# First stage of an encoder block: modulation weights loaded ahead of x, weight splits moved to VectorE, products of ones on TensorE

## The chip, the core and the metric

One core of a Trainium2 chip runs one launch of the kernel. The metric is the device time of one execution in microseconds, and the kernel before is given by the median of three: 2219.39 us (2219.05 to 2223.93).

TensorE multiplies matrices, VectorE, ScalarE and GpSimd (POOL in the profile) work elementwise, SyncE (SP) issues nearly all DMAs. Each engine takes its own instructions strictly in the order of the program and waits for the others by semaphores.

## The reference

A block of three residual steps on x (1024 tokens by 1024 channels, float32): a SwiGLU feed-forward, a mixer (chunked attention beside a recurrent branch), and a second SwiGLU feed-forward. Before each step x is normalised and modulated by a shift and a scale that come from a vector c:

```python
mod = (c_act @ w_ada[l] + b_ada[l]).reshape(b, N_SUB, 3, D_MODEL)
h = modulate(rmsnorm(x, g_pre), shift, scale)      # h * (1 + scale) + shift
g, u = jnp.split(h @ w_gu, 2, axis=-1)             # w_gu: 1024 x 5632
y = rmsnorm((jax.nn.silu(g) * u) @ w_down, g_post)
x = x + res_w * gate * y
```

Only the start of the first feed-forward is touched by the change: the first normalisation, the first shift and scale, and the first products with `w_gu`.

## The kernel before, in words

**Products in two halves.** A float32 operand is split into a high half (a cast to the matrix format, on ScalarE) and a low half (the operand less the high half, 128x1024 elements for a weight tile). `split` does this for weights, on VectorE or on GpSimd as its caller says. A product is then three matmuls of 128x512 (`mm3`, lines 465 to 467: high by high, low of x by high, high of x by low of the weight).

**The first stage** is `startup`. The feed-forward's gate and up matrices are cut into blocks of 128 columns. Block `fb` has two tiles, `(fb, 0)` for the gate and `(fb, 1)` for up, of 512 KB each; each is loaded (`load`) and split (`cut`). The 1024 channels of h are eight groups `k`, the tokens two halves `sh`. `part(fb, sh, k)` adds group k to two accumulators in PSUM: six matmuls. The first half of the tokens goes through blocks 0, 1 and 2 at the same time, so six accumulators are open, and there are six banks for them; two more banks (`trbank`) serve transposes and column products.

**One step k** of the stage needs, in this order:
- the x tiles 0 to 3 normalised: sum of squares on ScalarE (line 324), reciprocal root on GpSimd (325, 326), scaling on VectorE (1614) or, for tile 3, on ScalarE (1612);
- `trans`: four transposes on TensorE (line 1621) that put channel group k into a bank;
- the modulation weights of group k, `("a", k)`: 1 MB in four DMAs. `chain_seq` or `chain` sums them on VectorE, weighted by c (line 248 the first term, 250 the multiply-adds, 252 the sum of both halves); `mv` is a product with ones on TensorE (257) and two small VectorE operations (262, 265) that make the column of scale and shift;
- `h_act`: ScalarE writes the high half hh (341) and the full h (344); `h_lo`: VectorE makes the low half hl (336);
- `part` for the three blocks.

`startup` is under an order written out by hand for all five engines (`manual_schedule(engines=ALL_ENGINES)`): each engine keeps the order in which the program names its instructions, DMAs on SP included (`ld`). For k = 0 to 3 the order is written line by line; from then on a loop over j keeps VectorE two to three groups ahead of TensorE. The phases behind `startup` have orders by hand for the four computing engines or are left to a planner, which also places `skew_bias_rows` (line 1745) on SP.

**Where the weight splits go.** In `cut` the engine of the subtraction is chosen by block: GpSimd for blocks under `direct` (4 in the first feed-forward) and for block 1 of the second.

Of the kernel before, what the change touches and what calls it, by code (L numbers as in the profile page):

```python
# [23 lines left out]
P = 128  # L24
# [26 lines left out]
def kernel(  # L51
# [7 lines left out]
    nc = tc.nc  # L59
    x = x[0]  # L60
# [13 lines left out]
    def nm(s):  # L74
        cnt[0] += 1
        return f"{s}_{cnt[0]}"
# [15 lines left out]
    ones_r = cpool.tile([P, P], F32R, name="ones_r")  # L92
# [8 lines left out]
    def bank(name):  # L101
        return ps[0].tile([P, 512], F32, tag="ps", bufs=nbank[0], name=nm(name))
# [39 lines left out]
    def split(raw, hi, lo, eng=None):  # L142
        nc.scalar.copy(hi, raw)  # L143
        (eng or nc.vector).tensor_tensor(lo, raw, hi.bitcast(F32), op=ALU.subtract)  # L144
# [340 lines left out]
    def ffn(sub, w_gu, w_down, hh, hl, xin, xout):  # L485
# [4 lines left out]
        direct = DIRECT[sub]  # L490
# [27 lines left out]
        def cut(fb, i):  # L518
            if (fb, i) not in raws:
                return  # L520
            raw, spare = raws.pop((fb, i))
            shape = [P, KB, P]
            if spare:
                hi, lo = t4("sh", F32R, shape), t4("sl", F32R, shape)
            else:
                hi = wpool.tile(shape, F32R, tag="wh", bufs=4, name=nm("wh"))
                lo = wpool.tile(shape, F32R, tag="wl", bufs=4, name=nm("wl"))
            split(raw, hi, lo, nc.gpsimd if fb < direct and sub == 0 or fb == 1 else nc.vector)
            wts[fb, i] = hi, lo

        def part(fb, sh, k):
# [1057 lines left out]
    def startup(f1, hh, hl):  # L1589
        xt = [None] * SB  # L1590
        raws, wraw = {}, {}
        acc4 = tmp[0].tile([P, 2, 2, 2, P], F32, tag="gate", bufs=1, name=nm("acc4"))
        load_columns()

        def ld(*items):
            for it in items:
                if it[0] == "x":
                    xt[it[1]] = t4("x0")
                    nc.sync.dma_start(xt[it[1]], x[it[1] * P : (it[1] + 1) * P, :])
                elif it[0] == "a":  # L1600
                    raws[it[1]] = ada_load(it[1])
                else:
                    f1.load(it[1], it[2])

        rs = {}

        def mean_x(sb):
            rs[sb] = rstd_of(xt[sb], EPS)

        def norm_x(sb, on_act=False):  # L1610
            if on_act:
                nc.scalar.activation(xt[sb], xt[sb], AF.Copy, scale=rs[sb])
            else:
                nc.vector.tensor_scalar(xt[sb], xt[sb], rs[sb], None, op0=ALU.mult)

        tp = {}

        def trans(sh, k):
            pt = trbank("pt")
            for i in range(4):  # L1620
                nc.tensor.transpose(pt[:, i * P : (i + 1) * P], xt[sh * 4 + i][:, k * P : (k + 1) * P], ident)
            tp[sh, k] = pt

        def h_act(sh, k, on_act=True):
            return evac_h(0, sh, k, tp.pop((sh, k)), hh, hl, on_act, False)

        def h_lo(sh, k, h32):
            lo_h(sh, k, h32, hh, hl)

        def chain(j, half):  # L1630
            ada_sum(raws[j], acc4[:, j % 2], ((0, 4, 1, 5), (2, 6, 3, 7))[half])

        def chain_seq(j, half):
            ada_sum(raws[j], acc4[:, j % 2], range(4 * half, 4 * half + 4))

        def mv(j):
            ada_set(j, ada_mv(acc4[:, j % 2]))

        ld(("x", 0), ("x", 1), ("x", 2), ("x", 3), ("a", 0), ("w", 0, 0), ("w", 0, 1))
        ld(("a", 1), ("w", 1, 0), ("w", 1, 1), ("a", 2))  # L1640
        for sb in range(4):
            mean_x(sb)
        norm_x(0)
        norm_x(1)
        norm_x(2)
        norm_x(3, True)
        trans(0, 0)
        chain_seq(0, 0)
        chain_seq(0, 1)
        f1.cut(0, 0)  # L1650
        mv(0)
        trans(0, 1)
        h = h_act(0, 0)
        chain_seq(1, 0)
        h_lo(0, 0, h)
        chain_seq(1, 1)
        f1.cut(0, 1)
        f1.part(0, 0, 0)
        mv(1)
        f1.cut(1, 0)  # L1660
        h = h_act(0, 1)
        h_lo(0, 1, h)
        trans(0, 2)
        f1.part(0, 0, 1)
        ld(("w", 2, 0), ("w", 2, 1), ("a", 3), ("a", 4))
        f1.cut(1, 1)
        chain(2, 0)
        chain(2, 1)
        f1.part(1, 0, 0)
        mv(2)  # L1670
        h = h_act(0, 2)
        h_lo(0, 2, h)
        f1.part(1, 0, 1)
        trans(0, 3)
        ld(("a", 5))
        f1.cut(2, 0)
        chain(3, 0)
        chain(3, 1)
        f1.cut(2, 1)
        f1.part(0, 0, 2)  # L1680
        f1.part(1, 0, 2)
        mv(3)
        h = h_act(0, 3)
        ld(("a", 6))
        chain(4, 0)
        h_lo(0, 3, h)
        chain(4, 1)
        f1.part(2, 0, 0)
        f1.part(2, 0, 1)
        f1.part(2, 0, 2)  # L1690
        trans(0, 4)
        chain(5, 0)
        later = {3: [("a", 7), ("x", 4), ("x", 5)], 4: [("x", 6), ("x", 7)], 5: [("w", 3, 0)], 6: [("w", 3, 1)]}
        for j in range(3, KB):
            f1.part(0, 0, j)
            if j + 1 < KB:
                mv(j + 1)
                h = h_act(0, j + 1)
            ld(*later.get(j, ()))
            if j + 2 < KB:  # L1700
                chain(j + 2, 1)
            if j + 1 < KB:
                h_lo(0, j + 1, h)
            if j + 3 < KB:
                chain(j + 3, 0)
            if j in (3, 4):
                for sb in (2 * j - 2, 2 * j - 1):
                    mean_x(sb)
            if j in (4, 5):
                for sb in (2 * j - 4, 2 * j - 3):  # L1710
                    norm_x(sb, True)
            if j == 7:
                h_lo(1, 0, h_act(1, 0, True))
            f1.part(1, 0, j)
            f1.part(2, 0, j)
            if j + 2 < KB:
                trans(0, j + 2)
            else:
                trans(1, j - 6)
        f1.finish(0, 0, tu)  # L1720
        h_lo(1, 1, h_act(1, 1, True))
        trans(1, 2)
        for k in range(KB):
            f1.part(0, 1, k)
            if k + 2 < KB:
                h_lo(1, k + 2, h_act(1, k + 2, k % 2 == 0))
            if k < 2:
                f1.finish(k + 1, 0, tu)
            if k + 3 < KB:
                trans(1, k + 3)  # L1730
        f1.finish(0, 1)
        for fb in (1, 2):
            for k in range(KB):
                f1.part(fb, 1, k)
                f1.sum_step()
            f1.finish(fb, 1)
# [14 lines left out]
    with tc.tile_pool(name="psA", bufs=1, space=PSUM) as psA, tc.tile_pool(name="tmpA", bufs=1) as tmpA:  # L1751
        ps[0], tmp[0] = psA, tmpA
        with tc.manual_schedule(engines=ALL_ENGINES):
            hh, hl = new_h()
            f1 = ffn(0, ffn1_w_gu, ffn1_w_down, hh, hl, x, out if upto == 1 else x1)
# [68 lines left out]
```

## Time and profile before

| what | value |
|---|---|
| median of three executions | 2219.39 us (2219.05 to 2223.93) |
| the profiled execution | 2225.66 us |
| its span, first to last instruction | 2223.9 us |
| TensorE busy | 2155.0 us, 97% |
| VectorE, ScalarE, GpSimd busy | 60%, 46%, 33% |
| mean granted TensorE clock | 0.993 |
| TensorE waits over 9 us in the first 70 us | 9.3 us for `acc` |

The profiled execution is one of several, with the same order of work. Its span leaves out what lies ahead of the first instruction and behind the last. A row of groups names the source line, the engine, the operation, the tile written and the tiles read, the shape and the count; behind the first bar stand the busy time and the mean duration of one (in ns), behind the second the idle time of that engine just ahead and whom it waited for. A timeline row gives start and duration in us; "x4" merges four in a row. A matmul's duration is modelled and overlaps the next, so the spacing of two starts is what one costs.

### The profile page before, as it was taken

The numbers are of one execution on the slowest core, as the hardware profiler recorded it, in microseconds if no ns is written. First come the engines' busy times: TensorE is split into PE (matmuls) and PEld (weight loads), VectorE is DVE, ScalarE is ACT, GpSimd is POOL, SyncE is SP. The second block draws the span as 40 slices with busy tenths as digits, with TensorE's granted clock in tenths as the row PEclk, the third lists the DMA queues.
The fourth block names the chain that finished last, engine by engine and source line by source line (L and its number), as shares of the span: only waits on it lengthen the run. The fifth ranks groups of instructions, "written<-read, shape, count | busy, mean of one in ns | idle before, by whom it ended". The sixth has DMA issues, their size and how long they took to land. (4 is left out here: it accounts for less than half of the span.)

```text
span 2223.9 us, 26745 instructions
## 1 busy us (share of the span) xinstructions
PE 2155.0 (97%) x9963; PEld 1786.3 (80%) x9963; DVE 1324.4 (60%) x1704; ACT 1016.3 (46%) x1567; POOL 736.9 (33%) x530
## 2 busy tenths in 40 slices
PE   5999999999999999999999999999999999999998
PEld 3878788888878888888898988887788788888877
DVE  6686565558457677654236666556866564544455
ACT  3533333334446778711147777436443333334443
POOL 3458885422104111100121120003658793522102
PEclk9999999999999999999999999999999999999999
DMA  9437775449575111176411011464357653347375
GB/s 295 112 107 270 232 260 173 151 163 339 190 230 198 60 49 51 48 238 209 152 48 60 26 56 54 149 197 149 101 195 256 226 212 125 113 154 274 118 232 175
DMA packets 269594, 358.36 MB, mean 161 GB/s; under 512 B 16624, under 2 KB 178584, under 8 KB 269464
## 3 DMA queue, kind: packets, MB, share of 16 engines
q1 hardware_dynamic: 256680, 310.48, 43.2%
q10 hardware_dynamic: 12784, 46.18, 5.4%
q8 instruction: 78, 1.28, 0.2%
q14 instruction: 52, 0.43, 0.1%
HBM read 265.37 MB, written 94.37 MB: 162 GB/s over the span
## 5 line engine op out<-in xcount | busy, mean ns | idle before, releaser
L143 ACT CAST dh<-rawd 128x1024 fp32r<-128x1024 f32 x154 | 161.3, 1053 | 213.8 <-PE pv L899 72.8
L636 DVE TENSOR_TENSOR wm<-raw,wm 128x512 fp32r<-128x512 f32 x152 | 156.5, 1034 | 167.8 <-ACT wm L635 163.2
L144 DVE TENSOR_TENSOR dh<-rawd,dh 128x1024 fp32r<-128x1024 f32 x130 | 161.8, 1248 | 157.2 <-ACT dh L143 155.0
L466 PE MATMUL pj<-hl,wh 128*128 128x512 f32 x576 | 226.9, 394 | 5.7 <-DVE hl L336 5.7
L465 PE MATMUL pj<-hh,wh 128*128 128x512 f32 x576 | 229.4, 398 | 1.4 <-ACT wh L143 1.4
L467 PE MATMUL pj<-hh,wl 128*128 128x512 f32 x576 | 226.8, 394 | 0.7 <-DVE wl L144 0.7
L899 PE MATMUL px<-dh,dh 128*128 128x512 f32 x608 | 187.5, 390 | 1.2 <-DVE dh L144 1.1
L899 PE MATMUL pv<-dh,dh 128*128 128x512 f32 x528 | 165.4, 395 | 3.0 <-DVE dh L144 3.0
L325 POOL TENSOR_SCALAR rstd<-rstd 128x1 f32<-128x1 f32 x47 | 29.7, 632 | 408.7 <-ACT junk L324 407.3
L144 POOL TENSOR_TENSOR wl<-raw,wh 128x1024 fp32r<-128x1024 f32 x24 | 59.4, 2484 | 298.5 <-ACT wh L143 252.8
L143 ACT CAST wh<-raw 128x1024 fp32r<-128x1024 f32 (+1 forms) x86 | 86.7, 1010 | 146.3 <-DMA raw<-in_w_in_dram 42.7
L837 POOL TENSOR_TENSOR act<-act,act 128x512 f32<-128x512 f32 x54 | 87.0, 1611 | 162.1 <-DMA act<-act 123.2
L899 PE MATMUL px<-dh 128*128 128x512 f32 x352 | 137.3, 390 | 0.0
L899 PEld LDWEIGHTS px<-dh,dh 128*128 128x128 f32 x608 | 113.9, 188 | 25.8 <-DVE dh L144 2.3
L466 PEld LDWEIGHTS pj<-hl,wh 128*128 128x128 f32 x576 | 109.3, 190 | 29.6 <-DVE hl L336 7.7
L467 PEld LDWEIGHTS pj<-hh,wl 128*128 128x128 f32 x576 | 109.3, 190 | 24.7 <-DVE wl L144 1.9
L465 PEld LDWEIGHTS pj<-hh,wh 128*128 128x128 f32 x576 | 109.3, 190 | 23.4 <-ACT wh L143 1.8
L899 PEld LDWEIGHTS pv<-dh,dh 128*128 128x128 f32 x528 | 100.3, 191 | 25.1 <-DVE dh L144 4.3
L645 PE MATMUL psX<-hh,wm 128*128 128x512 f32 x296 | 116.0, 392 | 4.3 <-ACT mixes L668 4.3
L144 DVE TENSOR_TENSOR wl<-raw,wh 128x1024 fp32r<-128x1024 f32 (+1 forms) x62 | 71.3, 1153 | 78.4 <-ACT wh L143 78.4
L645 PE MATMUL psX<-hs,wm 128*128 128x512 f32 x296 | 115.9, 391 | 1.8 <-ACT mixes L661 1.7
L635 ACT CAST wm<-raw 128x512 fp32r<-128x512 f32 x152 | 92.7, 614 | 51.0 <-POOL raw L623 50.9
(310 smaller groups left out, 5770.6 us busy)
## 6 DMA issues: line engine op xcount, KB each, us to landing
rawa<-in_w_ada_dram SPq DMA_DIRECT2D x56, 512.0 KB, 4.8
raw<-in_ffn_w_gu_dram SPq DMA_DIRECT2D x49, 512.0 KB, 4.6
rawd<-acts SPq DMA_DIRECT2D x88, 256.0 KB, 4.1
rawd<-downs SPq DMA_DIRECT2D x88, 256.0 KB, 4.0
raw<-in_w_in_dram SPq DMA_DIRECT2D x44, 512.0 KB, 4.0
sr<-in_ffn_w_gu_dram SPq DMA_DIRECT2D x39, 512.0 KB, 6.3
act<-act SPq DMA_DIRECT2D x37, 512.0 KB, 5.3
acts<-act ACTq DMA_DIRECT2D x36, 512.0 KB, 3.7
```

What stands on the lines that cost most here:

```text
L143: nc.scalar.copy(hi, raw)
L144: (eng or nc.vector).tensor_tensor(lo, raw, hi.bitcast(F32), op=ALU.subtract)
L325: nc.gpsimd.tensor_scalar(r, r, eps, None, op0=ALU.add)
L465: nc.tensor.matmul(dst, wh[:, kk, :], xhk[:, sl], start=first, stop=False)
L466: nc.tensor.matmul(dst, wh[:, kk, :], xlk[:, sl], start=False, stop=False)
L467: nc.tensor.matmul(dst, wl[:, kk, :], xhk[:, sl], start=False, stop=last)
L635: nc.scalar.copy(t[:, 0], src)
L636: nc.vector.tensor_tensor(t[:, 1], src, t[:, 0].bitcast(F32), op=ALU.subtract)
L645: nc.tensor.matmul(dst, t[:, 0, kk, :], xh, start=first and kk == 0, stop=False, skip_group_check=True)
L837: nc.gpsimd.tensor_tensor(o, p, q, op=op)
L899: nc.tensor.matmul(dst, a_[:, 0, tk], w_[:, 1, :], start=first and n == 0, stop=last and n == 2, skip_group_check=True,)
```

## The change

Four edits, all in the start of the first feed-forward:
- **Loads.** The four DMAs of modulation group 0 are issued ahead of x tiles 0 to 3 instead of behind them.
- **Splits.** In the first feed-forward only block 3 keeps its subtraction on GpSimd; blocks 0, 1 and 2 go to VectorE. The second feed-forward's choice is as before (its block 1).
- **Products of ones.** `spin(n)` issues n matmuls of a 128x128 tile of ones with itself into a bank `idle` that nobody reads: 80 at the start, 8 behind each of the four transposes of group 0, and 8, 30, 8, 12 and 8 at five later places, 178 in all. The bank is one of the six; its last use is ahead of the first product of the accumulator that takes it.
- **Order.** The first chain goes ahead of the normalisation; `mv(0)` goes ahead of the transposes of group 0; chain 1 goes behind `part(0, 0, 0)`; casts and subtractions of the weight tiles (`cut`) move, those of block 2 to either side of `mv(3)`; `part(1, 0, 1)` goes ahead of `mv(2)`.

```diff
-            split(raw, hi, lo, nc.gpsimd if fb < direct and sub == 0 or fb == 1 else nc.vector)
+            split(raw, hi, lo, nc.gpsimd if (fb == 3 if sub == 0 else fb == 1) else nc.vector)
...
+        idle = bank("idle")
+
+        def spin(n):
+
+            for _ in range(n):
+                nc.tensor.matmul(idle[:, 0:P], ones_r, ones_r, start=True, stop=True)
+
+        def trans(sh, k, between=0):
             pt = trbank("pt")
             for i in range(4):
                 nc.tensor.transpose(pt[:, i * P : (i + 1) * P], xt[sh * 4 + i][:, k * P : (k + 1) * P], ident)
+                spin(between)
             tp[sh, k] = pt
...
-        ld(("x", 0), ("x", 1), ("x", 2), ("x", 3), ("a", 0), ("w", 0, 0), ("w", 0, 1))
+        ld(("a", 0), ("x", 0), ("x", 1), ("x", 2), ("x", 3), ("w", 0, 0), ("w", 0, 1))
         ld(("a", 1), ("w", 1, 0), ("w", 1, 1), ("a", 2))
+        spin(80)
+        chain_seq(0, 0)
+        chain_seq(0, 1)
         for sb in range(4):
             mean_x(sb)
-        norm_x(0)
-        norm_x(1)
-        norm_x(2)
-        norm_x(3, True)
-        trans(0, 0)
-        chain_seq(0, 0)
-        chain_seq(0, 1)
+        for sb in range(4):
+            norm_x(sb, sb == 3)
+        mv(0)
+        trans(0, 0, 8)
         f1.cut(0, 0)
-        mv(0)
         trans(0, 1)
         h = h_act(0, 0)
+        h_lo(0, 0, h)
+        f1.cut(0, 1)
+        spin(8)
+        f1.part(0, 0, 0)
+        spin(30)
         chain_seq(1, 0)
-        h_lo(0, 0, h)
         chain_seq(1, 1)
-        f1.cut(0, 1)
-        f1.part(0, 0, 0)
+        f1.cut(1, 0)
         mv(1)
-        f1.cut(1, 0)
         h = h_act(0, 1)
         h_lo(0, 1, h)
+        f1.cut(1, 1)
         trans(0, 2)
+        spin(8)
         f1.part(0, 0, 1)
         ld(("w", 2, 0), ("w", 2, 1), ("a", 3), ("a", 4))
-        f1.cut(1, 1)
         chain(2, 0)
         chain(2, 1)
         f1.part(1, 0, 0)
+        f1.part(1, 0, 1)
+        spin(12)
         mv(2)
         h = h_act(0, 2)
         h_lo(0, 2, h)
-        f1.part(1, 0, 1)
         trans(0, 3)
+        spin(8)
         ld(("a", 5))
-        f1.cut(2, 0)
+        f1.part(0, 0, 2)
+        f1.part(1, 0, 2)
         chain(3, 0)
         chain(3, 1)
-        f1.cut(2, 1)
-        f1.part(0, 0, 2)
-        f1.part(1, 0, 2)
+        f1.cut(2, 0)
         mv(3)
         h = h_act(0, 3)
+        f1.cut(2, 1)
+        h_lo(0, 3, h)
         ld(("a", 6))
         chain(4, 0)
-        h_lo(0, 3, h)
         chain(4, 1)
         f1.part(2, 0, 0)
         f1.part(2, 0, 1)
```

More of the change, by code (lines that the diff above doesn't have):

```diff
@@ L1616, in startup @@
         tp = {}
-        def trans(sh, k):
+        idle = bank("idle")
[3 more added lines that the diff above has]
+        def trans(sh, k, between=0):
             pt = trbank("pt")
```

## The prediction

> **What bounds the kernel now.** I read the page first, then who TensorE waits for, early and late.
>
> ```profile
> span 2223.9 us, 26745 instructions
> PE 2155.0 (97%) x9963; PEld 1786.3 (80%) x9963; DVE 1324.4 (60%) x1704; ACT 1016.3 (46%) x1567; POOL 736.9 (33%) x530
> ...
> L144 DVE TENSOR_TENSOR wl<-raw,wh 128x1024 fp32r<-128x1024 f32 (+1 forms) x62 | 71.3, 1153 | 78.4 <-ACT wh L143 78.4
> ```
>
> The waits of TensorE, first 70 us, then 70 to 300 us (total, times, longest):
>
> ```profile
> PE pcj L257 <- DVE acc L252: 9.3, 4, 4.9
> PE pt L1621 <- DVE x L1614: 7.5, 3, 5.0
> PE pj L466 <- DVE hl L336: 5.7, 3, 4.6
> ```
>
> ```profile
> PE psZ L645 <- ACT pp L672: 2.7, 2, 2.1
> ```
>
> TensorE is the bound except in the first 60 us, where it waits for VectorE: for the sums `acc` of modulation products, for the normalised x, for the low half `hl`. So the change is worth how much earlier TensorE gets into unbroken work. Groups of VectorE and GpSimd, 0 to 60 us:
>
> ```profile
> L250 DVE SCALAR_TENSOR_TENSOR acc<-rawa,c_act,acc 128x256 f32<-128x256 f32 x36 | 26.3, 771 | 0.4
> ```
>
> ```profile
> L144 POOL TENSOR_TENSOR sl<-sr,sh 128x1024 fp32r<-128x1024 f32 x2 | 5.0, 2508 | 6.3 <-ACT sh L143 6.3
> ```
>
> ```profile
> L250 DVE SCALAR_TENSOR_TENSOR acc<-rawa,c_act,acc x48: 473/479/2640, 12.7 to 70.0; 128x256 f32<-128x256 f32 x48
> ```
>
> The last row is the line's own view, with the shortest, median and longest of all its 48. A multiply-add has a median of 479 ns and a mean of 771 over the 36 that share the time with six GpSimd splits (2.5 us each): 36 x 0.29 = 10.5 us of VectorE are lost. The longest lost 2.1 us, about a split's own length, so five were each held up by one split, and the sixth split met none. In windows of 3.41 us (busy us of TensorE, its weight loads, VectorE, ScalarE and GpSimd, granted clock, DMA share, GB/s):
>
> ```profile
> 34.20:37.61 3.41, 3.11 (x8) 1.90 (x6) 3.38 (x7) 0.00 (x0) 0.75 (x1) 1.00 1.17 290
> ...
> 44.44:47.85 3.41, 0.00 (x0) 0.00 (x0) 3.41 (x5) 0.00 (x0) 1.81 (x1) 1.00 1.15 298
> 47.85:51.27 3.42, 2.55 (x8) 2.29 (x9) 2.21 (x8) 1.15 (x2) 0.00 (x0) 0.50 1.13 342
> 51.27:54.68 3.41, 3.41 (x9) 2.64 (x9) 3.12 (x9) 0.30 (x1) 0.00 (x0) 0.50 1.00 393
> 143.43:146.84 3.41, 1.72 (x8) 1.12 (x7) 3.41 (x3) 3.17 (x7) 2.75 (x2) 1.00 0.00 0
> ...
> 273.13:276.55 3.42, 1.32 (x7) 1.08 (x7) 1.80 (x2) 2.14 (x4) 3.34 (x3) 1.00 0.81 265
> 276.55:279.96 3.41, 3.41 (x10) 2.63 (x9) 3.05 (x4) 0.00 (x0) 3.33 (x3) 0.50 0.77 250
> ```
>
> After a window with TensorE busy 1.32 us of 3.41 (39%) the next runs at clock 0.50; after one with 1.72 (50%) it does not. A fully busy half-clock window brings full clock back. Before 37.6 us the clock column shows 1.00, but products start 0.43 us apart (24.85 to 25.28 in the timeline) as at 0.50 later, so I read the start as half clock too.
>
> **The change part by part.** The timeline of before (start, duration):
>
> ```profile
> 3.31 0.39 PE L124 MATMUL pa<-ident,rowsA 96*128 96x96 f32 x1 [0.61 <-DMA rowsA<-in_norm_pre_dram]
> ...
> 10.53 1.06 ACT L324 ACTIVATE junk<-x 128x1024 bf16<-128x1024 f32 x1 [0.21 <-DMA x<-in_x_dram]
> ...
> 12.29 0.35 DVE L248 TENSOR_SCALAR acc<-rawa,c_act 128x256 f32<-128x256 f32 x1 [0.23 <-DMA rawa<-in_w_ada_dram]
> ...
> 14.02 0.47 PE L1621 MATMUL pt<-ident,x 128*128 128x128 f32 x1 [1.43 <-ACT x L1612]
> ...
> 16.10 0.42 DVE L252 TENSOR_TENSOR acc<-acc 128x256 f32<-128x256 f32 x1
> ...
> 17.97 1.11 PE L1621 MATMUL pt<-ident,x 128*128 128x128 f32 x4 [0.38 <-DVE scol L265]
> 18.01 0.78 ACT L341 ACTIVATE hh<-pt,scol,acol 128x512 fp32r<-128x512 f32 x1 [1.09 <-DVE scol L265]
> 18.69 0.77 ACT L344 ACTIVATE h<-pt,scol,acol 128x512 f32<-128x512 f32 x1
> ...
> 19.35 1.04 ACT L143 CAST wh<-raw 128x1024 fp32r<-128x1024 f32 x1
> ...
> 23.52 0.69 DVE L336 TENSOR_TENSOR hl<-h,hh 128x512 fp32r<-128x512 f32 x1
> ...
> 24.85 0.63 PE L467 MATMUL pj<-hh,wl 128*128 128x512 f32 x1
> ...
> 25.28 0.63 PE L465 MATMUL pj<-hh,wh 128*128 128x512 f32 x1
> ...
> 31.50 0.69 DVE L336 TENSOR_TENSOR hl<-h,hh 128x512 fp32r<-128x512 f32 x1 [1.57 <-ACT h L344]
> ...
> 37.25 0.42 DVE L252 TENSOR_TENSOR acc<-acc 128x256 f32<-128x256 f32 x1
> 38.43 0.22 DVE L262 SCALAR_TENSOR_TENSOR acol<-pcj,colsA 128x1 f32<-128x1 f32 x1 [0.76 <-PE pcj L257]
> ...
> 40.29 0.69 DVE L336 TENSOR_TENSOR hl<-h,hh 128x512 fp32r<-128x512 f32 x1 [1.58 <-ACT h L344]
> ```
>
> ```profile
> 48.15 0.42 DVE L252 TENSOR_TENSOR acc<-acc 128x256 f32<-128x256 f32 x1
> ...
> 49.75 0.22 DVE L262 SCALAR_TENSOR_TENSOR acol<-pcj,colsA 128x1 f32<-128x1 f32 x1 [1.17 <-PE pcj L257]
> ...
> 51.60 0.69 DVE L336 TENSOR_TENSOR hl<-h,hh 128x512 fp32r<-128x512 f32 x1 [0.26 <-ACT h L344]
> ...
> 56.16 0.60 PE L1621 MATMUL pt<-ident,x 128*128 128x128 f32 x4
> ...
> 56.52 0.47 PE L465 MATMUL pj<-hh,wh 128*128 128x512 f32 x1
> ...
> 56.83 0.39 PE L466 MATMUL pj<-hl,wh 128*128 128x512 f32 x1
> 57.05 0.39 PE L467 MATMUL pj<-hh,wl 128*128 128x512 f32 x1
> ```
>
> *Loads.* SP issues the four DMAs of the first modulation block (1.05 MB) ahead of the x tiles instead of behind them. At 290 GB/s that is 3.6 us, so the square of x tile 3 starts at 10.5 + 3.6 = 14.1, and its transpose 3.5 us later (14.02 less 10.53), at 17.6. Everything behind these eight transfers lands as before.
>
> *First chain.* The block is in by 7 or 8 (the 2.1 MB of x behind it, at 290 GB/s or somewhat more, end at 14.1). `chain_seq(0)` (4.2 us, 12.29 to 16.52) is done by about 11, ahead of the normalisation on VectorE, and the first column is set beside it. Step 0 is now held by x, not by the sum: ScalarE ends the last normalisation at about 17.6, casts the first weight (1.04) to 18.6, then makes hh and h (18.01 to 19.46 = 1.45) to 20.1. `hl` is done at 20.8 against 24.2, since it no longer stands behind the blocked half chain.
>
> *Splits.* Six subtractions move from GpSimd (2.5 us each) to VectorE: 6 x 1.15 = 6.9 us added there, 10.5 us of blocking gone: 3.6 us net. Where they stand decides what of it counts. Step by step, VectorE's queue being the path:
> - weight (0,1): cast 20.1 to 21.1, low half to 22.3. Chain 1 (4.2) to 26.5.
> - low half (1,0) to 27.7, which hides the column product on TensorE (0.8, from 37.67 to 38.43); column set (0.3, two small operations) to 28.0; h at 29.5; `hl` 30.2 against 32.2. Gain 2.0.
> - cast and low half (1,1) to 31.7. Chain 2 was 5.5 us (32.2, where `hl` ends, to 37.7) with one add held up; 3.4 without. Chain 3 was 7.6 (41.0 to 48.6) with two; 3.4 too. So chain 2 ends at 35.1. Product and column (0.8 + 0.3) bring 36.2, h 37.7, `hl` 38.4 against 41.0. Gain 2.6.
> - chain 3 to 41.8 against 48.6; low half (2,0) to 42.9; column 43.2 against 50.0; h 44.75. Then ScalarE casts (2,1), which stood far ahead before, to 45.75, VectorE subtracts to 46.9 and only then makes `hl` to 47.6 against 52.3. Gain 4.7.
>
> *TensorE.* The three parts of block 2 (18 products) come next. Five run before (2,1) is there at 46.9; 13 are left. TensorE has only these five and the column product between about 41.8 and 46.9, so I take one window at half clock, by the 39% row: 8 products at 0.43 and 5 at 0.23 (56.83 to 57.05) end at 51.5, the transposes (0.45) at 51.95. The part that started at 56.5 then starts at 52.0: **gain 4.5 us**. From there TensorE is unbroken, and the order is the old one; the next low half is due about 57.2 and VectorE has it by about 57.1.
>
> *Products of ones.* 178 products of 128 moving columns, on TensorE alone, into the bank that the sixth accumulator takes up later (same engine, no new wait by the order). No row shows them. A quarter of the 512-column spacing is 0.107 us cold and 0.057 full; the transposes of the same size are 0.21 ((1.11 - 0.47)/3) and 0.11. Eighty from 3.7 us (3.31 + 0.39) end at 11.5 or at about 15.7, if full clock comes near 10; the 24 between transposes end by 14 or 19. The last transpose is due at 17.6 and ScalarE casts until 18.6: cost 0 to 0.7 us; I take 0, since the spacing of the 512-column rows fits the column count. The 30 before column 1 (22.6 to 24.3 or 26.0) lie under chain 1, which ends at 26.5. Their return is that the 12 products at 31 to 34 and the transposes run at full clock and stay off the path. Left uncovered, the 30 would cost up to 6.4 at 0.21.
>
> By the 273.13 row a window that is 39% busy is enough for half clock, and the sum goes by that. [...]
>
> **Sum.** The profiled execution took 2225.66, 1.8 us more than its span, and is 6.3 above the median of 2219.39; the lost time is early and the same in each. 2219.4 - 4.5 = **2214.9 us** (span 2219.4 for an execution like the profiled one).
>
> **The rivals.**
> - *Clock stays full* through 41 to 51: the 13 products at 0.23 end at 49.9, the part starts at 50.4, 6.1 us gained, **2213.3**. [...] For: the windows' place is free, and two half-empty windows may both keep over half. Against: the 273.13 row. A quarter.
> - *Half clock earlier*: if the window near 27 to 31 (columns, transposes, two products waiting for `hl`) falls under half, 18 products from 29 run mostly at 0.43 and column 2, due at 35.1, waits for them until 38 to 40. Two to four us of the 4.5 go: about **2218**. For: the thin filling there. Against: 38 products of ones stand around it. 0.15.
> - *Passed on to later waits*: TensorE gains nothing if a later stage is set by something that does not shift, as DMA or the planner's order of the later, unfixed parts: **2219**. For: 2.7 us of waits for ScalarE at the next stage. Against: that chain starts from `hl` and shifts too. 0.11.
> - *Slower: the ones hold the queue.* If they cost 0.21 throughout and never bring full clock, 80 end at 20.5, the column product at 21.3, 27 more starts at 27.0, and hh starts some 9 us late; the 30, behind a part that ends near 31.5, end near 37.8 and hold column 1, due 35.5, for 2 more. 11 - 4.5 = 6.5 lost, and more with cold products behind: about **2227**. It decides from a mean of 0.12 us ((17.6 - 3.7 - 0.8)/107) on. For: the transposes' price. Against: any busy window has brought the clock back in the rows. 0.06.
>
> **How the numbers follow.** The forecast has 0.43. A measurement tells about 0.3%, 6.7 us, from no change. Faster than that: under half of the first rival, and the forecast's edge where later half-clock windows (1.7 us each) fall away: 0.16. Slower: the last rival and a little of the third: 0.08. Same: 0.76. The range 2210 to 2222 takes in the first three rivals and such windows either way; the forecast's own is 2212 to 2217.
>
> **What would show it.** GpSimd splits gone from the first 60 us and no multiply-add over 0.5 us; the square of x 3 near 14.1; `hl` starting at about 20.1, 29.5, 37.7, 46.9; one half-clock window between 44 and 53; the first part of block 0 behind block 2's three at 52. Wrong, if the transposes of step 0 come after 19, if products of ones start over 0.12 apart, or if the start is 4 us early and the end is not.

## The result, and the profile after

The changed kernel takes **2226.84 us** (median; 2222.29 to 2230.4) against 2219.22 beside it: a ratio of **1.0033, 95% interval 1.0024 to 1.0042**. It is 7.6 us slower, a third of a per cent, and the interval does not reach 1. The forecast was 2214.9, with a range of 2210 to 2222. The case that came is the last rival, "the ones hold the queue", which had 0.06 and a price of about 2227.

The head of the page of the changed kernel:

```profile
span 2228.6 us, 27099 instructions
...
PE 2182.4 (98%) x10141; PEld 1816.6 (82%) x10141; DVE 1326.9 (60%) x1710; ACT 1016.3 (46%) x1567; POOL 720.4 (32%) x524
```

TensorE is busy for 27 us more than before, and its waits in the first 70 us look cured (total, times, longest):

```profile
PE pj L465 <- ACT sh L143: 2.2, 1, 2.2
PE pt L1627 <- DVE scol L265: 0.8, 2, 0.4
PE pcj L257 <- DVE acc L252: 0.6, 1, 0.6
PE pj L466 <- DVE hl L336: 0.5, 1, 0.5
```

The 9.3, 7.5 and 5.7 us of before have shrunk to 0.6, 0.8 and 0.5. That is not time gained: TensorE does not wait because it is still at the ones, and the wait is on the other engines. The timeline of the changed kernel (line 1622 are the ones, line 1627 the transposes that were line 1621):

```profile
3.40 17.31 PE L1622 MATMUL idle<-ones_r 128*128 128x128 f32 x80
...
11.07 0.42 DVE L252 TENSOR_TENSOR acc<-acc 128x256 f32<-128x256 f32 x1
...
14.28 1.06 ACT L324 ACTIVATE junk<-x 128x1024 bf16<-128x1024 f32 x1 [0.15 <-DMA x<-in_x_dram]
...
20.51 0.95 PE L257 MATMUL pcj<-ones_r,acc 128*128 128x1 f32 x4
21.32 0.45 PE L1627 MATMUL pt<-ident,x 128*128 128x128 f32 x1
21.43 1.95 PE L1622 MATMUL idle<-ones_r 128*128 128x128 f32 x8
...
26.84 0.43 PE L1627 MATMUL pt<-ident,x 128*128 128x128 f32 x1
...
27.32 0.78 ACT L341 ACTIVATE hh<-pt,scol,acol 128x512 fp32r<-128x512 f32 x1 [8.18 <-PE pt L1627]
28.80 0.69 DVE L336 TENSOR_TENSOR hl<-h,hh 128x512 fp32r<-128x512 f32 x1 [5.88 <-ACT h L344]
...
33.82 4.25 PE L1622 MATMUL idle<-ones_r 128*128 128x128 f32 x30
34.64 0.43 DVE L252 TENSOR_TENSOR acc<-acc 128x256 f32<-128x256 f32 x1
37.91 0.55 PE L257 MATMUL pcj<-ones_r,acc 128*128 128x1 f32 x4
38.40 5.33 SPq L1756 DMA_DIRECT2D relrep<-in_rel_rows_dram  x8
```

The sum for column 0 is ready at 11.5 (11.07 + 0.42), and its product starts at 20.51, behind 80 ones of 0.21 us each. The four transposes follow with eight ones behind each, to 26.84; ScalarE has waited 8.18 us for the last. The sum for column 1 is ready at 35.07, and its product comes at 37.91, behind the 30. Up to `psX` the granted clock of this trace is 0.50 from 38.9 to 45.7 us and from 59.4 to 62.8, and changes only at the ends of windows of 3.41 us. Some of these windows (columns as in the prediction: busy us of the five engines, granted clock, DMA share, GB/s):

```profile
4.76:8.17 3.41, 3.41 (x18) 3.41 (x17) 1.81 (x4) 0.00 (x0) 0.00 (x0) 1.00 0.92 282
8.17:11.58 3.41, 3.41 (x18) 3.41 (x17) 2.23 (x5) 1.15 (x2) 0.01 (x1) 1.00 1.02 414
...
14.99:18.40 3.41, 3.41 (x18) 3.41 (x17) 0.75 (x1) 1.79 (x4) 1.85 (x3) 1.00 1.14 287
...
35.47:38.88 3.41, 3.03 (x28) 2.95 (x27) 1.02 (x3) 0.00 (x1) 0.00 (x0) 1.00 1.17 290
38.88:42.29 3.41, 3.41 (x14) 3.23 (x15) 1.69 (x2) 2.38 (x3) 0.00 (x0) 0.50 1.14 312
42.29:45.70 3.41, 3.41 (x9) 2.64 (x8) 3.38 (x10) 0.00 (x0) 0.00 (x0) 0.50 0.94 256
```

The four windows from 4.76 to 18.40 hold 18 matmuls each, all of them ones (those that reach over an edge are counted on both sides): the spacing, 0.21 us (17.31 / 80), stays what it was at the start. (The clock column shows 1.00 there, but before its first change it can't be taken at its word: behind 35.47 the ones come 0.11 us apart.) So 17 us of ones without a gap did not raise the clock. The spacing falls to 0.11 us only behind products with weights, at 35.47: of the 30 ones, 8 run in the 1.65 us before it, and 22 in the 2.6 us behind it. And that window, 89% busy by the record, is followed by 0.50, as is the next, which is fully busy by the record.

The part of step 3, which started at 56.52 before, starts here at 64.98:

```profile
51.27 0.69 DVE L336 TENSOR_TENSOR hl<-h,hh 128x512 fp32r<-128x512 f32 x1 [1.58 <-ACT h L344]
...
60.30 0.68 DVE L336 TENSOR_TENSOR hl<-h,hh 128x512 fp32r<-128x512 f32 x1
...
64.63 0.60 PE L1627 MATMUL pt<-ident,x 128*128 128x128 f32 x4
64.98 0.48 PE L465 MATMUL pj<-hh,wh 128*128 128x512 f32 x1
```

The first product of the next phase (`psX`, line 645) starts at 147.33 against 138.83: 8.5 us late at both marks. What lies behind takes 2077.7 us (2226.84 less 1.8 around the span, less 147.33; the median is used, since single profiles differ by several us behind this mark), and 2078.6 before by the same working. So the loss is there at 65 us, and nothing is added behind `psX`.

### The profile page after: what moved, and what is told of

Same layout as the page of the kernel before. It is cut to its first block, busy times and chain, and to the rows that moved or that the text cites. A ratio compares the mean times of both kernels' runs of the same rounds, so it can differ in the third digit from the quotient of the medians.

```text
span 2228.6 us, 27099 instructions
## 1 busy us (share of the span) xinstructions
PE 2182.4 (98%) x10141; PEld 1816.6 (82%) x10141; DVE 1326.9 (60%) x1710; ACT 1016.3 (46%) x1567; POOL 720.4 (32%) x524
## 5 line engine op out<-in xcount | busy, mean ns | idle before, releaser
L325 POOL TENSOR_SCALAR rstd<-rstd 128x1 f32<-128x1 f32 x47 | 30.7, 652 | 450.4 <-ACT junk L324 438.6
L144 POOL TENSOR_TENSOR wl<-raw,wh 128x1024 fp32r<-128x1024 f32 x22 | 54.7, 2495 | 293.0 <-ACT wh L143 248.4
```

## The experiments

All twelve stand in one table, since they are read against one another: when the part of step 3 starts, when `psX` starts, the time, and the ratio to the kernel before that ran beside each (2219.2 to 2220.9 us).

| kernel | part of step 3 | `psX` | time, us | ratio (95%) |
|---|---|---|---|---|
| before | 56.52 | 138.83 | 2219.22 | 1 |
| after | 64.98 | 147.33 | 2226.84 | 1.0033 (1.0024, 1.0042) |
| no_ones | 55.21 | 137.93 | 2218.08 | 0.9991 (0.9982, 1.0000) |
| wide_ones | 52.86 | 137.63 | 2218.02 | 0.9988 (0.9979, 0.9997) |
| bf16_ones | 53.59 | 139.18 | 2220.85 | 1.0001 (0.9991, 1.001) |
| ones_256 | 52.41 | 137.15 | 2219.2 (one run) | |
| loads_only | 60.67 | 142.96 | 2224.05 | 1.0016 (1.0007, 1.0025) |
| gps_no_ones | 61.00 | 143.36 | 2224.86 | 1.0024 (1.0015, 1.0034) |
| splits_only | 47.08 | 137.17 | 2218.8 | 0.9989 (0.9978, 1.0) |
| rows_last | 55.42 | 137.71 | 2220.73 | 1.0006 (0.9994, 1.0017) |
| splits_rows_last | 47.07 | 129.39 | 2216.41 | 0.9976 (0.9966, 0.9985) |
| splits_rows_mid | 48.31 | 130.59 | **2210.86** | **0.9959 (0.9945, 0.9973)** |
| wide_rows_mid | 53.95 | 136.26 | 2216.7 | 0.9989 (0.998, 0.9998) |
| splits_ones_mid | 47.39 | 129.66 | 2212.17 | 0.9965 (0.9953, 0.9978) |

The two marks come from one profile of each kernel, and carry about 1 us of its own. The square of x tile 3 starts at 10.53 in the profile of before, but in that of rows_last, whose edit concerns later transfers only, at

```profile
9.57 1.06 ACT L324 ACTIVATE junk<-x 128x1024 bf16<-128x1024 f32 x1 [0.18 <-DMA x<-in_x_dram]
```

(9.66 in splits_only), and rows_last is then 1.1 us ahead of before at both marks without being faster at the end. In the same way x tile 3 comes 1.0 us later in no_ones (15.26) than in the changed kernel and in wide_ones (14.28 and 14.26). Leads of about 1 us at a mark say nothing.

### The ones taken out, made wider, or made narrower in type

**no_ones**: the changed kernel without the 178 products of ones, which nothing reads.

```diff
-            for _ in range(n):
-                nc.tensor.matmul(idle[:, 0:P], ones_r, ones_r, start=True, stop=True)
+            pass
```

> The changed kernel without its 178 products of ones; loads, splits and order as changed. Theory A (the ones, at 0.21 us each, hold TensorE's queue and cost all of the loss; the rest of the change is a gain as forecast): the first low half hl starts near 20.1 us (28.8 with the ones, 23.5 before), the first part behind block 2's three near 53 (65.0 with, 56.5 before), the time 2215 to 2217 us. Rival B (x behind the modulation block, or the splits on VectorE, cost by themselves): hl later than 23 or that part later than 56, the time 2219 us or more.

Measured: the part of step 3 at 55.21, 9.8 us earlier than with the ones, and 2218.08 us, 8.8 less. The ones alone make the loss: without them the change is hardly to be told from the kernel before (0.9991, interval up to 1.0000). Both theories missed in part. The ones cost all of the loss, but the rest is no gain of the size forecast: the part starts at 55.2, not near 53. Low halves start at 21.4, 30.7, 40.5 and 49.5, against 28.8, 40.4, 51.3 and 60.3 with them.

**wide_ones**: each four ones become one product of 512 moving columns (the same tile of ones read four times over; "moving" is the operand whose columns are counted here, "stationary" the other, here called its weights; the profile records its load on PEld, at 3.30 us for the first of these products, which starts at 3.39).

```diff
+        ones_w = ones_r.unsqueeze(1).to_broadcast([P, 4, P])
...
-            for _ in range(n):
-                nc.tensor.matmul(idle[:, 0:P], ones_r, ones_r, start=True, stop=True)
+            for _ in range((n + 3) // 4):
+                nc.tensor.matmul(idle.rearrange("p (a n) -> p a n", n=P), ones_r, ones_w, start=True, stop=True)
```

> The changed kernel with every four products of ones of 128 columns made into one of 512 (the same ones read four times over; 20, 2, 2, 2, 2, 2, 8, 2, 3, 2 in place of 80, 8, 8, 8, 8, 8, 30, 8, 12, 8). Theory A1 (a 128-column product takes 0.21 us because its weight load is as long as its stream, the array streams half the time, and that half is what keeps the clock down): starts 0.43 us apart, full clock granted by about 10 us, then 0.23 apart, the 20 over by about 10 us, the stage unhindered, 2212 to 2216 us. Rival A2 (products of ones never count for the clock, whatever their length, or no work raises it in the first 30 us): 0.43 apart throughout, the 20 over at 12, no full clock before 30 us, 2215 to 2219 us.

Its timeline and windows:

```profile
3.39 6.24 PE L1623 MATMUL idle<-ones_r 128*128 128x512 f32 x20
```

```profile
3.04:6.46 3.42, 3.16 (x8) 2.59 (x9) 0.91 (x4) 0.00 (x0) 0.00 (x0) 1.00 0.88 231
6.46:9.87 3.41, 3.18 (x14) 2.25 (x12) 2.10 (x5) 0.00 (x0) 0.00 (x0) 1.00 0.95 334
9.87:13.28 3.41, 0.66 (x5) 0.58 (x6) 2.20 (x5) 2.68 (x5) 1.25 (x3) 1.00 1.03 398
13.28:16.70 3.42, 3.02 (x8) 1.58 (x9) 1.70 (x4) 1.92 (x4) 2.89 (x5) 0.50 1.16 296
```

The same number of moving columns is done at 9.6 instead of 20.7. Eight products fit the window to 6.46 and fourteen the next: 0.426 us each, then 0.227. The clock is up after one window, and is lost again at 13.3, behind a window that is 19% busy. This run shows what the prediction's own working was worth: it forecast low halves at 20.1, 29.5, 37.7 and 46.9 and the part at 52.0; here they start at 20.43, 29.63, 39.01 and 48.04, and the part at 52.86. The time, 2218.02, is above the expected 2212 to 2216. Of the 3.7 us of lead at that mark 1.2 are left at `psX`; among ScalarE's waits from 46 to 100 us stands the reason:

```profile
ACT junk L324 <- DMA x<-in_x_dram: 3.9, 1, 3.9
```

It waits for x tile 4, on which more below.

**bf16_ones**: the count stays at 178 and the columns at 128, but both operands are read as bf16 (the bytes of the ones, so their values are another pattern; nothing reads the product).

```diff
+        ones_b = ones_r.bitcast(BF16)[:, 0:P]
...
-                nc.tensor.matmul(idle[:, 0:P], ones_r, ones_r, start=True, stop=True)
+                nc.tensor.matmul(idle[:, 0:P], ones_b, ones_b, start=True, stop=True)
```

> The changed kernel with its 178 products in bfloat16 (the same bytes read as bfloat16, so zeros and ones in turn), 128 columns as before. Theory A1 with a weight load that goes by the width of the element: starts about 0.107 us apart at half clock, full clock by about 10 us, the 80 over by 12, 2212 to 2217 us. If the weight load is as long as in float32: 0.21 apart, no full clock, about 2227 us as in the changed kernel. Rival A2: 0.107 apart but no full clock before 30 us, 2216 to 2220 us.

```profile
3.44 6.50 PE L1623 MATMUL idle<-ones_r 128*128 128x128 bf16 x80
```

```profile
3.92:7.33 3.41, 3.41 (x35) 3.41 (x33) 1.42 (x5) 0.00 (x0) 0.00 (x0) 1.00 0.97 260
7.33:10.75 3.42, 2.61 (x46) 2.43 (x43) 1.87 (x5) 0.15 (x1) 0.00 (x0) 1.00 1.00 384
```

The 80 are done at 9.9. They come 0.107 us apart to 7.3 and 0.056 behind it. That is the price that the prediction gave to the float32 ones. For bf16 it fits the count of moving columns (0.107 is a quarter of the 0.426 of 512 columns); the 0.213 of the float32 ones does not. The time, 2220.85, is that of before and not the 2212 to 2217 expected: the planner puts six transfers of the bias rows ahead here (see below), ScalarE waits 4.7 us for x tile 4, and the lead of 2.9 us at step 3 is gone at `psX`.

**ones_256**: each two ones become one of 256 columns, to tell the load of the stationary tile from the stream of the moving one.

```diff
+        ones_w = ones_r.unsqueeze(1).to_broadcast([P, 2, P])
...
-            for _ in range(n):
-                nc.tensor.matmul(idle[:, 0:P], ones_r, ones_r, start=True, stop=True)
+            for _ in range((n + 1) // 2):
+                nc.tensor.matmul(idle[:, 0 : 2 * P].rearrange("p (a n) -> p a n", n=P), ones_r, ones_w, start=True, stop=True)
```

> The changed kernel with each two ones of 128 columns made one of 256 columns. Theory (the ones' price is the loading of their 128 columns of float32 weights, not the columns that move, and a stream with gaps of that kind does not raise the clock): each costs about 0.213 us at first, the load just covers with the stream, the clock is full by 7 to 10 us, and 40 of them end at 9 to 10; the step-3 part starts near 53. Rival (no number of columns under 512 raises the clock): 0.213 throughout, 40 end near 12, and the clock stays at half until the products with weights come.

```profile
3.26 7.69 PE L1623 MATMUL idle<-ones_r 128*128 128x256 f32 x40
```

```profile
5.93:9.35 3.42, 3.42 (x18) 3.42 (x17) 2.28 (x6) 0.00 (x0) 0.00 (x0) 1.00 0.96 323
9.35:12.76 3.41, 2.21 (x18) 1.92 (x16) 2.29 (x5) 2.40 (x5) 1.00 (x3) 1.00 1.02 405
```

The window to 9.35 holds 18 products and 17 loads, exactly as with 128 columns: twice the columns cost the same 0.21 us. Behind it they come 0.11 us apart. So the spacing of the narrow ones is not set by their columns. What sets it is not shown: the loads fill the record of that window (17 in 3.42 us), but so do those of the bf16 ones (33 in 3.41), and no run times a load by itself. In both float32 kernels the row says 3.41 or 3.42 us busy; in one the clock rises at 9.35, in the other not in 17 us of ones.

### The loads and the order

**loads_only**: the kernel before, with the four transfers of the first modulation group ahead of x.

```diff
-        ld(("x", 0), ("x", 1), ("x", 2), ("x", 3), ("a", 0), ("w", 0, 0), ("w", 0, 1))
+        ld(("a", 0), ("x", 0), ("x", 1), ("x", 2), ("x", 3), ("w", 0, 0), ("w", 0, 1))
```

> The kernel before with one edit: modulation group 0's DMAs ahead of x tiles 0 to 3. Theory I (in the old order VectorE takes the first chain behind the normalisation, so with x some 3.6 us later the first column is 2 to 3.5 us later): first low half hl at 25 to 27 us instead of 23.5, part of step 3 at 57 to 60, 2220 to 2223 us. Rival J (the chain's later data are already there, so hl is not later): part of step 3 at 56 to 57, 2218 to 2220 us.

Measured: the last transpose of step 0 starts at 17.97 against 14.02, the first chain, which stands behind x, ends at 22.07 against 16.52, the part of step 3 starts at 60.67 against 56.52, and the time is 2224.05 us, 3.2 over the 2220.90 beside it and a little beyond what was expected. The delay of x goes through to the end.

**gps_no_ones**: loads and order of the changed kernel, no ones, the splits on GpSimd as before.

```diff
-            split(raw, hi, lo, nc.gpsimd if (fb == 3 if sub == 0 else fb == 1) else nc.vector)
+            split(raw, hi, lo, nc.gpsimd if fb < direct and sub == 0 or fb == 1 else nc.vector)
...
-            for _ in range(n):
-                nc.tensor.matmul(idle[:, 0:P], ones_r, ones_r, start=True, stop=True)
+            pass
```

> The changed kernel without the products of ones and with the splits back on GpSimd, so loads and order alone. Theory K (the new order is worth nothing by itself: chain 1 and the splits stand later than before): multiply-adds of up to 2.6 us are back, part of step 3 at 57 to 62 us against 55.2 with the splits on VectorE, 2220 to 2226 us. Rival L (the order carries a gain of its own): that part before 55.5, under 2218 us.

Measured: the part of step 3 at 61.00, 2224.86 us. TensorE waits for a split on GpSimd again (1.30 us, at 55.36). The new order does not win back what the loads cost. What lies behind the start of `psX` takes 2077.7 to 2081.2 us in every kernel here but splits_rows_last, so parts can be compared at that mark. Going from kernel to kernel, one part at a time, the 8.5 us fall into loads +4.1 (142.96 less 138.83), order +0.4, splits -5.4 (137.93 less 143.36) and ones +9.4 (147.33 less 137.93). Such steps add up in any case, each has the 1 us named above, and another sequence would share them out otherwise: the splits by themselves bring 1.7 at this mark, as the next run shows.

### The splits alone, and what became of their gain

**splits_only**: the kernel before, with the splits of blocks 0 to 2 on VectorE.

```diff
-            split(raw, hi, lo, nc.gpsimd if fb < direct and sub == 0 or fb == 1 else nc.vector)
+            split(raw, hi, lo, nc.gpsimd if (fb == 3 if sub == 0 else fb == 1) else nc.vector)
```

> The kernel before with one edit: the subtractions of weight blocks 0 to 2 on VectorE instead of GpSimd; loads and order as before, no ones. Theory C (VectorE loses 10.5 us to GpSimd's splits and pays 6.9 for its own): no multiply-add over 0.5 us, the part that started at 56.5 starts at 52 to 55, 2215 to 2218 us. Rival D (in the old order the added subtractions stand on the path and the removed blocking was partly covered): that part at 56 or later, 2219 to 2221 us.

Three views of it: the line of the multiply-adds, TensorE's timeline at step 3, and the timeline of ScalarE and SP behind it:

```profile
L250 DVE SCALAR_TENSOR_TENSOR acc<-rawa,c_act,acc x48: 474/479/486, 11.9 to 67.0; 128x256 f32<-128x256 f32 x48
```

```profile
47.08 0.48 PE L465 MATMUL pj<-hh,wh 128*128 128x512 f32 x1
```

```profile
37.55 2.76 SPq L1745 DMA_DIRECT2D relrep<-in_rel_rows_dram  x4
40.42 11.88 SPq L239 DMA_DIRECT2D rawa<-in_w_ada_dram  x8
52.39 2.19 SPq L1599 DMA_DIRECT2D x<-in_x_dram  x4
...
57.91 1.06 ACT L324 ACTIVATE junk<-x 128x1024 bf16<-128x1024 f32 x1 [6.98 <-DMA x<-in_x_dram]
60.23 0.76 ACT L341 ACTIVATE hh<-pt,scol,acol 128x512 fp32r<-128x512 f32 x1
```

No multiply-add is held up any more (longest 486 ns against 2640), and the part of step 3 starts 9.4 us earlier, well ahead of the 52 to 55 expected. Of the 9.4, 2.6 come behind the low half of step 3 (from there to the part 2.3 us against 4.9): before is at half clock from 47.85 to 54.68, while the products of splits_only stay 0.23 us apart up to 56.5 and are 0.43 apart from 63.03. Yet `psX` is only 1.7 earlier and the time 2218.8. The gain is lost at 51 to 58: ScalarE waits 6.98 us for x tile 4, and the high half of the next group stands behind that square. The tile is late because the planner, which places `skew_bias_rows` on SP, puts four of its eight transfers (0.38 MB each) ahead of the last modulation groups and of x; in the kernel before it was one of eight, with seven behind x.

**rows_last** and **splits_rows_last** move the call of `skew_bias_rows` into the order by hand, behind `startup`, without and with the splits.

```diff
             startup(f1, hh, hl)
-        skew_bias_rows()
+            skew_bias_rows()
```

> The kernel before with one edit: the eight DMAs of the bias rows fixed behind the stage's own DMAs. Theory F: the stage before never waited for the transfers behind them, so nothing changes: 2218 to 2221 us. Rival H (these DMAs cost or save time by themselves, early or late): under 2216 us or over 2222.

> The kernel before with two edits: the subtractions of blocks 0 to 2 on VectorE, and the eight DMAs of the bias rows (383 KB each) fixed behind the stage's own DMAs on SP instead of where the planner puts them. Theory F (with splits alone the stage was 9.4 us ahead at step 3 and lost most of it because the planner let four of these DMAs in ahead of modulation groups 6 and 7 and of x tiles 4 to 7, and ScalarE waited 7.0 us for x tile 4): ScalarE waits under 1 us for x tile 4, block 0's part of step 3 still starts near 47 us, and the lead of some 9 us over the kernel before reaches the end: 2210 to 2212 us. Rival G (the lead is lost to something else, as VectorE's own rate per step): the wait for x is gone but the time stays at 2215 to 2219 us.

Measured: rows_last is no different from before (1.0006). Against rows_last, whose transfers are in the same order, splits_rows_last is 8.4 us ahead at step 3 (55.42 less 47.07), which is the better measure of the splits. It keeps its lead of 9.4 us over before to `psX`, but ends at 2216.41, not at 2210 to 2212: 4.5 us under the 2220.90 beside it. 6.6 are lost behind `psX` (2085.2 from there on, by the working above, against 2078.6 in before and 2081.2 in rows_last). Its transfers now go out at 124 us, and the views of that place show what they meet (the waits of all engines from 140 to 165 us, then the window behind):

```profile
124.39 5.19 SPq L1745 DMA_DIRECT2D relrep<-in_rel_rows_dram  x8
```

```profile
POOL wsum L623 <- DMA act<-a: 10.8, 1, 10.8
```

```profile
143.40:146.81 3.41, 1.19 (x6) 0.65 (x4) 0.00 (x0) 0.30 (x1) 3.18 (x4) 1.00 1.01 401
146.81:150.22 3.41, 2.55 (x6) 2.07 (x7) 3.06 (x3) 1.85 (x4) 3.33 (x3) 0.51 1.09 337
150.22:153.63 3.41, 3.41 (x9) 2.63 (x9) 1.97 (x3) 0.00 (x0) 3.25 (x3) 0.50 0.43 114
```

GpSimd waits 10.8 us for a transfer of the next phase, TensorE's window at 143 is 35% busy, and two windows at half clock follow. 3 MB must go somewhere, and both places tried so far have other transfers due.

**splits_rows_mid** puts them between: inside the first stage, behind the last weight tile that it loads, at 52.6 us.

```diff
             ld(*later.get(j, ()))
+            if j == 6:
+                skew_bias_rows()
...
             startup(f1, hh, hl)
-        skew_bias_rows()
```

> The splits of blocks 0 to 2 on VectorE alone, with the eight transfers of the bias rows issued by hand inside the first stage, behind the last weight tile that it loads. Theory (the splits' 9.4 us are lost again only where those transfers stand ahead of x tile 4 or beside the next stage's loads): the part of step 3 starts near 47.1, ScalarE does not wait for x tile 4 for more than 1 us, the lead is still 8 to 9.5 us at 160 us, and the time is 2210 to 2213 us. Rival (the later phases are not set by the first stage at all): the lead is there at 160 us but the time stays at 2216 to 2219.

```profile
35.68 9.45 SPq L239 DMA_DIRECT2D rawa<-in_w_ada_dram  x10
45.23 3.10 SPq L1599 DMA_DIRECT2D x<-in_x_dram  x4
52.59 7.94 SPq L1747 DMA_DIRECT2D relrep<-in_rel_rows_dram  x8
```

```profile
52.04 1.05 ACT L324 ACTIVATE junk<-x 128x1024 bf16<-128x1024 f32 x1
```

Measured: no wait ahead of the square of x tile 4; 8.2 us of lead at step 3, 8.2 at `psX`, and **2210.86 us, 0.9959 (0.9945 to 0.9973)**, 8.7 us less than the 2219.59 of before beside it and 16 less than the changed kernel. So the gain of one line of the change passes to the end once these transfers are out of its way.

**wide_rows_mid** and **splits_ones_mid** ask whether ones are worth having. The first is wide_ones with the transfers so placed. The second is splits_rows_mid with 254 bf16 ones where TensorE waits.

```diff
+        spin(80)
+        trans(0, 0, 18)
...
+        spin(40)
         f1.part(0, 0, 0)
...
+        spin(8)
         f1.part(0, 0, 1)
...
+        spin(24)
         mv(2)
...
+        spin(30)
         mv(3)
```

> The changed kernel with 512-column ones (each four of 128 columns made one), and the bias rows placed by hand inside the first stage as in the run beside it. Theory (of the 3.7 us that 512-column ones leave at step 3, 2.5 are lost to the wait for x tile 4): the lead of 3.7 is kept behind it, and the time is 2215 to 2217 us, 2 to 3 under the same kernel without this placement. Rival (what is lost there is lost to the other order): 2218.

> The splits on VectorE and the bias rows inside the first stage, as in the first run of this call, and 254 bf16 products of ones put only where TensorE stands idle for other engines there (80 ahead of the first transpose, 18 behind each of the four, 40, 8, 24 and 30 at the four places where it waits for the low half or the column). Theory (VectorE's chain sets the steps, so that the clock matters only for transposes and columns): the clock is full from about 7.5 us, each low half comes 0.3 to 1 us earlier than without the ones, the part of step 3 starts near 45.5 to 46.5, and the time is 0.5 to 2 us under the run without ones. Rival (the ones delay a column or a product by overrunning their place): the part of step 3 starts at 47 or later and the time is not lower.

Measured: wide_rows_mid has no wait for x tile 4 and keeps its lead from mark to mark, but the lead is 2.6 us and not the 3.7 expected, and its 2216.7 (0.9989) is within the measurement of wide_ones' 2218.02 (0.9988): a gain at the end is not shown here. splits_ones_mid has full clock before 10 us (18 of its ones take 1.17 us from 9.48) and leads splits_rows_mid by 0.9 us at both marks, no more than one profile differs from another, and its time of 2212.17 is no lower; the intervals overlap. Forty of its ones overran (19.70 to 23.95, ahead of a product that started at 18.33 without them), and its first weight tile landed 1.3 us later, which may not be due to them. Ones gain nothing measurable here, cheap or not.

## Why the prediction was wrong

**The step that failed** is the price of the ones, and with it the clock that they were to bring: "I take 0, since the spacing of the 512-column rows fits the column count". They cost 0.21 and 0.11 us, the transposes' price, not 0.107 and 0.057, and "if full clock comes near 10" did not come true: the ones left the clock where it was until 35.5. The clock weighs more. At the transposes' price but with full clock near 10 the working itself had the 80 done at about 15.7 and a cost of 0.7 at most, and ones_256 shows a float32 stream of that spacing that does bring the clock up at 9.35. At half clock throughout, the 80 held the first column product from 11.5 to 20.51 and the 30 the second from 35.07 to 37.91; no_ones is 9.8 us ahead at step 3.

Both prices stood in the working, and I chose by type of work (products) where the row of the same shape, 128 columns with a float32 stationary tile, was the nearer one. By ones_256, the 512-column rows (0.426 us) hide whatever holds the narrow ones back, since it is as long as 256 columns (0.213).

The rival that I gave 0.06 had the account right, nearly to the tenth: 80 done at 20.5 (20.7), column product at 21.3 (21.46), last transpose at 27.0 (26.84), the 30 done near 37.8 (38.07), total 2227 (2226.84). The point from which it decides, 0.12 us, was not tested: no run has a price between 0.107 and 0.213. My argument against it, that "any busy window has brought the clock back in the rows", was drawn from products of 512 columns only. Its reading "A fully busy half-clock window brings full clock back" does not hold for recorded busy time in the changed kernel: the window at 38.88 is 3.41 us busy at half clock, and the next is at 0.50 again.

**The rest of the sum**, read from wide_ones, where the ones cost what I took: the low halves within 0.3 us for the first two and 1.3 for the others, the part of step 3 at 52.86 for 52.0. The square of x tile 3 came at 14.28 for 14.1. No multiply-add is over 0.5 us in the changed kernel (473 to 486 ns for all 48), and in splits_only, where the splits alone leave GpSimd, the longest goes from 2640 to 486 ns, so the blocking by GpSimd was real. Of "one half-clock window between 44 and 53" wide_ones has the one (products 0.43 us apart from 48.77 to 50.48, 0.23 from 50.88 on), but the clock of 0.50 from 13.28 to 16.70 ahead of it too; the changed kernel has others (38.88 to 45.7, 59.4 to 62.8). A slip of a tenth in the working (43.2 and 1.45 make 44.65, not 44.75) changes nothing.

**A second step failed out of sight.** "Everything behind these eight transfers lands as before": the planner moved the bias rows ahead (eight at 38.40 in the changed kernel, one before). In the changed kernel itself no wait for x tile 4 follows, since the steps are late anyway. But with the ones at the price that I gave them (wide_ones), ScalarE waits 3.9 us for it. So even with cheap ones the sum would have been out by 2.5: this is "passed on to later waits", through SP's order, which I had named as "DMA" without asking what would move.

**What the sum hid.** The net of 4.5 us came near what wide_ones shows at step 3 (3.7), but by luck, from parts that were off both ways: the splits, which the working priced at "3.6 us net" of VectorE's time, bring 8.4 to 9.4 by themselves, and the loads, which it made part of an early first step, cost 4.1. The ledger had `hl` of step 0 early (20.8 done against 24.2) by the loads and the new order together. It starts at 20.52 in gps_no_ones, with loads and order and the splits on GpSimd, at 20.55 in splits_only, with neither, and at 25.20 in loads_only. So either the order or the splits bring that gain, the loads do not, and both together bring it only once (20.43 in wide_ones). What the loads and the new place of chain 1 do besides is to end chain 1 at 26.7 (wide_ones) rather than 23.5 (splits_only).

Two things stay open. Loads and order together cost 4.5 us at `psX`, though the first chain no longer stands behind x there; how much of that is x and how much the place of chain 1 was not taken apart. And single profiles differ by several us behind `psX`: 2085.1 us from there in the profile of before, whose mean granted clock is 0.993, and 2076.3 in that of no_ones, at 0.996. From these means I estimate 31 and 18 us at half clock in the whole span ((1 - 0.993) x 2223.9 x 2, and the like), and the 13 us between them might be worth some 6 of the 8.8, at 0.43 and 0.23 us a product. But rows_last and splits_only are both at 0.993 and differ by 5.5, so it is not the whole; the comparisons go by medians.

## What to carry to other kernels

Price a filler product by a row of its own shape and type, and look in the trace whether it brings the clock that it is there for: here float32 products of 128 columns cost the same 0.21 us as those of 256, and only the wider ones raised the clock (at 9.35). Count waits that vanish from the bottleneck engine as a gain only if the engines behind it move too. An early gain reaches the end only if every transfer due in the time saved is issued in time: look who places the DMAs that nobody waits for yet, and put them by hand where nothing else is due. Try each part of a change alone; here one line of it, with eight transfers put in their place, took 8.7 us off where the whole added 7.6.

## What the runs showed of the hardware

**In these runs the records' busy time did not decide the clock.** For these types and widths, spacing at half and full clock, and whether the clock rose:

| product of ones | half clock, us | full clock, us | clock full from |
|---|---|---|---|
| float32, 128 columns (after) | 0.213 | 0.110 | not in the 17 us of the 80 |
| float32, 256 columns (ones_256) | 0.213 | 0.11 | 9.35 |
| float32, 512 columns (wide_ones) | 0.426 | 0.227 | 6.46 |
| bf16, 128 columns (bf16_ones) | 0.107 | 0.056 | 7.33 |

The first two rows have the same spacing, the same operand and windows that are fully busy by the record (3.41 and 3.42 us), and differ in the columns that move. My estimate is that the share of the time in which columns move divides the kinds. It takes from the bf16 row that 128 columns move in 0.107 us at half clock, half of 0.213, and in 0.056 at full clock.

The same estimate fits four more windows, but not a fifth. At 35.47 in the changed kernel the 22 ones at full clock move columns for 22 x 0.056 = 1.2 us, 36% of the window, below the 39% of the row at 273.13 of before that also lost the clock, though the record says 89%. At 38.88 twelve narrow products at 0.107 and two of 512 columns at 0.43 make 2.1 us, 62%, and the clock stays at half. The window of ones_256 from 2.52 to 5.93, with ones from 3.26, makes 78% and does not raise it; that of wide_ones from 3.04 to 6.46, with ones from 3.39, makes 90%, and does. But the window from 32.05 to 35.47 in the changed kernel, with 512-column products up to 33.82 and eight ones behind them, makes 77%, and the clock rises. So it gives no limit. It is worked out from the spacings above and the counts of these windows; no run measured the share itself.
